# Loading the first expert group ahead of the routing, its rows from ranks alone, and a shorter last job in a two-block kernel

## The chip, the cores and the metric

The kernel runs on one core of one Trainium2 chip. The metric is device time in microseconds (us). The kernel before takes 1078.39 us, the median of 3 runs (1076.84 to 1080.43). The engines are named as in the profile: PE is TensorE (PEld its weight loads), DVE is VectorE, ACT is ScalarE, POOL is GpSimd, SP is SyncE, which here issues nearly all transfers ("SPq" is its queue). TensorE's clock is shown as a share of full speed: 1.0 is 2.4 GHz and 0.5 is 1.2 GHz.

## The reference, cut to what matters

Two blocks run one after the other on 256 tokens of 1024 channels, everything in float32. The first (retention, gated recurrence, feed-forward) is not touched. The second is a mixer and a mixture of 32 experts:

```python
def second_block(x, ...):
    h = h + hybrid_mixer(rms_norm(h, norm1_g), ...)   # mLSTM half and gMLP half, then y @ w_out
    h = h + hierarchical_moe(rms_norm(h, norm2_g), ...)
    return rms_norm(h, final_g)

def hierarchical_moe(xn, w_rg, b_rg, w_re, b_re, w_gate, w_up, w_down):
    g_sel = argmax(softmax(xf @ w_rg + b_rg))            # 1 of 4 groups per token
    top_p, top_i = top_k(softmax(le of that group), 2)   # 2 of its 8 experts
    weights = p_gsel * top_p / sum(top_p)
    # per expert: (silu(x @ w_gate) * (x @ w_up)) @ w_down, times the weight, summed per token
```

The mixer's output is the concatenation of an mLSTM part (y_m) and a gMLP part (y_g), multiplied by w_out (1024 x 1024). Each expert has w_gate and w_up of 1024 x 512 and w_down of 512 x 1024, 6 MiB together; all 32 make 192 MiB.

## The kernel before, in words

**The mixer's last product (proj8, L316).** w_out is walked in 8 units of 24 products (L331). Each unit's weights come as a raw tile and are split into a high part (whi, on ACT, L159) and a low part (wlo, on DVE, L165), so that three fast products give float32 accuracy; `unit` (L204) makes the splits of the units ahead before its own products, with 4 whi and 3 wlo buffers. Units 0 to 3 use the y_m half. In the middle of unit 3 PE transposes the y_g half (`mid_yg`, L1316, transposes L1236). Its evacuation into a high and a low part (ACT L1244, DVE L1245) is called before unit 4 (`before_wo`, L1320), so behind the splits of unit 4 on ACT's queue. Engines run their queues in program order.

**The routing (L1425 to L1530).** From the logits, chains of small DVE steps pick the group and two experts of each token (EB marks them, L1452). PE counts: `ranks` (L1413) gives each token's rank inside its expert, `counts` the tokens per expert. DVE turns counts into an order of experts (key, then c_pos, their place), PE spreads the places over tokens (L1461), and the "name" of a token's row (512 times place, plus rank) is summed into DD (L1466, L1468) and DB (L1522). `choose` (L1502, L1503) makes a 0/1 matrix of a group's names, and `gather` multiplies it with the normalised tokens (L1510) to line up the rows of a group. Only later `r_ids` (L1539 to L1541) writes IDS, the experts' numbers in order of place, which the transfers need.

**The expert jobs.** Places 28 to 31 belong to experts 0 to 3 whatever the counts (STAT, "static"); the other 28 experts are sorted and known only through IDS. `slot_groups` makes 10 groups of 128 rows, most of four experts with 32 rows. A group g has six jobs: (g, 0) to (g, 3) multiply by w_gate and w_up (`gate_up`, L1627), (g, 4) and (g, 5) by the two column halves of w_down (`down`, L1647) and add to the residual (e0, e1: L1656, L1657, L1663 to L1665). Group 0 holds the four static experts. The jobs stand in the order (0,0) (0,1) (0,2) (0,3) (1,0) (0,4) (0,5) (1,1) ...

**The loads.** One load is one expert's share of one job, 1 MiB. `loads` (L1004) lists them in the order of the jobs: 16 static loads for (0,0) to (0,3), and then (1,0), which needs IDS. `ex` (L1030) issues them in that order and stops at the first load that has no buffer or no IDS yet. There are 18 buffers at the start (L1018 to L1026): four raw2, FR2, FR3, xg, yy, lb, five raw, FR1, two pairs of whi, one pair of wlo. xg and yy are used once, the others again as soon as a job has read them. The last job (9,5) is cut in two halves of 256 columns, whose loads are cut too; each half reads 256 of every 512 columns, that is runs of 1 KiB (L1064, L1065). In the last job the products go part by part (L1646), and `e0`, `e1` split the result in high and low parts.

**Side work.** `chain` queues small steps; after each job `advance(3)` takes one step of each of the first three chains that may run. "rows" has six steps (name rows and weights by token), and "flag" and "fing" (final gain rows) follow prep1.

Of the kernel before, what the change touches and what calls it, by code (L numbers as in the profile page):

```python
# [22 lines left out]
T = 256  # L23
# [16 lines left out]
HOLD = 5  # L40
HOLD_AT, OVER_AT = (3, 1), (3, 2)
# [56 lines left out]
def _build(tc, nc, h, out, ctx, dbg, stop):  # L98
# [105 lines left out]
    def unit(mm, stages=(), n=1, before=None, tag=None):  # L204
# [111 lines left out]
    def proj8(xh, xl, stages, before=None, n=1, mid=None):  # L316

        ps = {}
        for i in range(8):
# [15 lines left out]
            unit(mm, st_, n, before=(before or {}).get(i), tag=("p8", i - 4) if i >= 4 else None)  # L335
# [668 lines left out]
    loads = [(p, c) for g, c in jobs for p in keys[g]]  # L1004
# [25 lines left out]
    def ex(n=len(loads)):  # L1030

        while est["n"] < min(n, len(loads)):
# [27 lines left out]
            w = 2048 // len(t)  # L1060
            for j, b in enumerate(t):
                y = src[:, j * w:j * w + w]
                if (x, c) in last:
                    f = slice(256, 512) if half else slice(0, 256)  # L1064
                    y, b = [z.rearrange("p (m c) -> p m c", c=512)[:, :, f] for z in (y, b)]  # L1065
                SP.dma_start(b, y, cond=has)
# [8 lines left out]

    def raw_of(x, c):
# [5 lines left out]
        return lambda a, b: cols_of(eraw[i], a, b)  # L1082
# [194 lines left out]
    def logits(i):  # L1277

        p = lg["p"]
        for m in (2 * i, 2 * i + 1):  # L1280
# [4 lines left out]
    def squares_of(i):  # L1285

        for t in range(2):
            for j in range(2):
# [27 lines left out]
    def mid_yg():  # L1316
        need("yg")
        yt[0]()

    def before_wo(i):  # L1320
        def f():
            ex(RING2 + 2)
            if i == 4:
                yt[1]()
                yt[2]()
# [6 lines left out]
          mid={(3, 2): mid_yg, (7, 2): mid_wo})  # L1332
# [46 lines left out]
    onB = PD.tile([128, 128], BF16, name="onB")  # L1379
    w1, w2, gs = [sc[:, :, i] for i in range(3)]  # L1380
    DD = PD.tile([128, 4], F32, name="DD")
    d1, d2 = DD[:, 0:2], DD[:, 2:4]
    LGg, LGe = LG[:, :, 0:4], LG[:, :, 8:40]
# [11 lines left out]
    dg = H1[:, 4:6, 0:T]  # L1395
# [17 lines left out]
    def ranks(p):  # L1413

        for n, (a, b, c) in enumerate(((triB, 0, 0), (onB, 0, 32), (triB, 1, 32))):
            PE.matmul(p[:, c:c + 32], a, EB[:, b], start=n == 0, stop=False, skip_group_check=True)
# [6 lines left out]


    G.tensor_tensor(triB, tri, ident, op=OP.subtract)  # L1425
    G.memset(onB, 1.0)
    V.tensor_tensor(sqt2[0], sqt2[0], sqt2[2], op=OP.add)
    hs[3][0](lg["h"])
    S.activation(sqt2[3], HT3, AF.Square)
    squares_of(0)  # L1430
    logits(3)
# [554 lines left out]
```

## Time and profile before

| what | value |
|---|---|
| median of 3 runs | 1078.39 us |
| the profiled execution | 1078.93 us, its span 1077.2 us |
| granted PE clock, mean | 0.954 |
| busy share of the span | PE 90%, PEld 71%, DVE 49%, ACT 38%, POOL 7% |
| bytes in the records of transfers, bytes read by the HBM counter | 294.96 MB, 305.16 MB |

The page's three rows on the span, in 40 equal slices (26.9 us each), in which the digits are tenths:

```
PE   6999999999999999999999987999588778878765
PEclk9999999999999999999999988999799988989888
DMA  8545453346456555554664739999999999999994
```

Up to slice 24 PE is busy throughout and the transfers about half of the time; from there to the end the transfers are at their full rate and PE has gaps. In a timeline row stand the start, the time, the engine, the line, the operation, output and inputs, the number of records merged, and in brackets the idle time ahead and what ended it. A float32 product appears as two records.

### The profile page before, as it was taken

The numbers are of one execution on the slowest core, as the hardware profiler recorded it, in microseconds if no ns is written. First come the engines' busy times: TensorE is split into PE (matmuls) and PEld (weight loads), VectorE is DVE, ScalarE is ACT, GpSimd is POOL, SyncE is SP. The second block draws the span as 40 slices with busy tenths as digits, with TensorE's granted clock in tenths as the row PEclk, the third lists the DMA queues.
The fourth block names the chain that finished last, engine by engine and source line by source line (L and its number), as shares of the span: only waits on it lengthen the run. The fifth ranks groups of instructions, "written<-read, shape, count | busy, mean of one in ns | idle before, by whom it ended". The sixth has DMA issues, their size and how long they took to land.

```text
span 1077.2 us, 19357 instructions
## 1 busy us (share of the span) xinstructions
PE 972.0 (90%) x7815; PEld 763.7 (71%) x7815; DVE 532.7 (49%) x961; ACT 405.8 (38%) x675; POOL 71.1 (7%) x59
## 2 busy tenths in 40 slices
PE   6999999999999999999999987999588778878765
PEld 6999998899999999999978964545244424424322
DVE  6787784476777666567877533313112202112012
ACT  6567954366465544445486431111001000100002
POOL 2037500010000000000200000000000000000001
PEclk9999999999999999999999988999799988989888
DMA  8545453346456555554664739999999999999994
GB/s 334 187 165 185 144 195 115 111 154 208 184 195 218 192 195 176 178 195 162 229 234 154 317 127 418 417 413 417 412 420 417 415 421 417 417 419 417 416 407 152
DMA packets 51482, 294.96 MB, mean 274 GB/s; under 512 B 5429, under 2 KB 11189, under 8 KB 20666
## 3 DMA queue, kind: packets, MB, share of 16 engines
q1 hardware_dynamic: 51096, 293.25, 70.1%
q8 instruction: 64, 1.05, 0.4%
q10 hardware_dynamic: 290, 0.39, 0.2%
q14 instruction: 32, 0.26, 0.1%
HBM read 305.16 MB, written 1.05 MB: 284 GB/s over the span
## 4 chain that ended last, share of the span: by engine, by line
PE 62%; DMA 30%; DVE 4%; ACT 1%; issue 1%; SPq 1%; ACTq 0%; DVEq 0%
PE mm L227 42%; DMA raw<-in_we_dram 13%; DMA FR<-in_we_dram 7%; DMA whi<-in_we_dram 6%; PE mm L331 4%; PE sa L1627 3%; PE mm L1647 3%; DMA wlo<-in_we_dram 2%; PE tp L1510 2%; DMA lb<-in_we_dram 2%; PE tp L227 1%; DVE wlo L165 1%; DMA XS<-in_xt_dram 1%; PE sa L227 1%; PE tp L511 0%
## 5 line engine op out<-in xcount | busy, mean ns | idle before, releaser
L227 PE MATMUL mm<-FR,whi 128*128 128x256 f32 (+1 forms) x2080 | 380.6, 285 | 9.1 <-ACT FR L268 8.0
L227 PEld LDWEIGHTS mm<-FR,whi 128*128 128x128 f32 x2080 | 323.4, 190 | 11.9 <-ACT FR L268 8.0
L165 DVE TENSOR_TENSOR wlo<-raw,whi 128x1024 fp32r<-128x1024 f32 x188 | 243.9, 1300 | 139.6 <-PE mm L227 72.0
L227 PE MATMUL mm<-FR,wlo 128*128 128x256 f32 (+1 forms) x1040 | 295.3, 284 | 0.8 <-DVE wlo L165 0.8
L159 ACT ACTIVATE whi<-raw 128x1024 fp32r<-128x1024 f32 x190 | 200.3, 1059 | 201.7 <-PE mm L227 142.2
L227 PEld LDWEIGHTS mm<-FR,wlo 128*128 128x128 f32 x1040 | 198.0, 190 | 1.0 <-DVE wlo L165 1.0
L1627 PE MATMUL sa<-raw,xg 128*32 128x256 f32 (+1 forms) x1200 | 150.6, 426 | 19.5 <-DMA raw<-in_we_dram 19.5
L1627 PEld LDWEIGHTS sa<-raw,xg 128*32 128x32 f32 (+1 forms) x1200 | 73.2, 126 | 56.4 <-DMA raw<-in_we_dram 27.2
L1647 PE MATMUL mm<-raw,ht 128*32 128x512 f32 (+2 forms) x328 | 73.0, 638 | 14.3 <-DMA raw<-in_we_dram 14.3
L1627 PE MATMUL sa<-FR,xg 128*32 128x256 f32 (+1 forms) x416 | 71.6, 426 | 15.7 <-DMA FR<-in_we_dram 15.7
L1638 ACT ACTIVATE ht<-tp 128x128 f32<-128x128 f32 x40 | 11.1, 278 | 173.5 <-PE tp L1637 173.5
L1627 PE MATMUL sa<-whi,xg 128*32 128x256 f32 (+1 forms) x256 | 67.8, 422 | 2.6 <-DMA whi<-in_we_dram 2.6
L1657 DVE SCALAR_TENSOR_TENSOR yy<-mm,ws,yy 128x512 fp32r<-128x512 f32 (+1 forms) x21 | 15.2, 724 | 110.2 <-ACT yy L1656 110.2
L1665 DVE TENSOR_TENSOR XS<-mm,XS 128x512 f32<-128x512 f32 (+1 forms) x42 | 26.0, 661 | 84.5 <-PE mm L1664 84.5
L1627 PEld LDWEIGHTS sa<-FR,xg 128*32 128x32 f32 (+1 forms) x416 | 33.2, 126 | 36.2 <-DMA FR<-in_we_dram 20.7
L1647 PEld LDWEIGHTS mm<-raw,ht 128*32 128x32 f32 (+1 forms) x328 | 18.4, 122 | 56.9 <-issue 28.6
L1633 DVE TENSOR_TENSOR sg<-sg,sa 128x128 f32<-128x128 f32 x40 | 11.3, 283 | 81.2 <-ACT sg L1632 81.2
L227 PE MATMUL mm<-FL,whi 128*128 128x256 f32 x176 | 49.9, 284 | 0.0
L331 PE MATMUL mm<-FR,whi 128*128 128x256 f32 x256 | 48.5, 290 | 1.6 <-ACT FR L1244 1.4
L227 PE MATMUL mm<-FH,wlo 128*128 128x256 f32 x176 | 49.8, 283 | 0.0
L227 PE MATMUL mm<-FH,whi 128*128 128x256 f32 x176 | 49.8, 283 | 0.0
L1510 PE MATMUL tp<-qm,FR 128*128 128x256 f32 (+1 forms) x192 | 42.9, 377 | 1.8 <-DVE qm L1503 1.8
(427 smaller groups left out, 1400.1 us busy)
## 6 DMA issues: line engine op xcount, KB each, us to landing
raw<-in_we_dram SPq DMA_DIRECT2D x106, 1024.0 KB
raw<-in_wd_dram SPq DMA_DIRECT2D x94, 1024.0 KB
FR<-in_we_dram SPq DMA_DIRECT2D x35, 1024.0 KB
whi<-in_we_dram SPq DMA_DIRECT2D x44, 512.0 KB
lb<-in_we_dram SPq DMA_DIRECT2D x12, 1024.0 KB
wlo<-in_we_dram SPq DMA_DIRECT2D x22, 512.0 KB
raw<-in_we_dram SPq DMA_DIRECT2D x4, 512.0 KB
raw<-in_wd_dram SPq DMA_DIRECT2D x2, 512.0 KB
```

The source lines that it names most:

```text
L159: S.activation(his[u], half(u), AF.Copy)
L165: (G if u in POOL_LO or u - 2 * nch in POOL_LO else V).tensor_tensor(los[u], half(u), his[u].bitcast(F32), op=OP.subtract)
L227: PE.matmul(o, a, b, start=start and i == 0, stop=stop and i == 2)
L331: PE.matmul(p[:, j * T:j * T + T], w[:, b:b + 128], z[:, k, 0:T], start=k == 0 and j == 0 and x == 0, stop=k == 7 and x == 2, skip_group_c ...
L1510: PE.matmul(p[:, kk * 256:kk * 256 + w], XN[:, t, k * 128:k * 128 + 128], qm[:, t, 0:w], start=t == 0, stop=t == 1)
L1627: PE.matmul(p[r, 0:256], x[:, k, r], raw(k * 256, k * 256 + 256), start=k == 0, stop=k == 7)
L1633: V.tensor_tensor(sg[:, 128:256], sg[:, 0:128], p[:, 128:256], op=OP.mult)
L1638: S.activation(ht()[:, c], q[:, 0:128], AF.Copy)
L1647: PE.matmul(p[r, 0:n], ht[:, m, r], raw(m * 512 + a, m * 512 + a + n), start=m == 0, stop=m == 3)
L1657: V.scalar_tensor_tensor(yl, p[:, 0:n], ws[:, 0:1], yh.bitcast(F32), OP.mult, OP.subtract)
L1665: V.tensor_tensor(HB[:, t, c0:c0 + n], o[:, 0:n], HB[:, t, c0:c0 + n], op=OP.add)
```

## The change

It has these parts. (1) **Load order**: the four static loads of (0,4) are moved ahead of (1,0); the order of the jobs stays. (2) **First group's rows from ranks alone**: the places of the static experts are constants (BS), so PE adds them to the ranks directly, and `names` makes the row names of group 0 in DS before places are known; keys, places and the names of the other groups follow behind the first matrices (`places` ahead of the first gather product, `places_mm` after the second), and the first group's gathered rows are all evacuated by ACT. (3) **Unread products**: `turn` lets PE multiply 128 x 256 constants into a tile that nobody reads, three times ahead of the ranks and twice behind the counts. (4) **gMLP part**: `mid_yg` also evacuates the y_g half, and unit 3 leaves the splits of its last unit ahead (`defer`) until after its products. (5) **End of w_out**: the last addition, square and logits go in two halves. (6) **Name rows in three steps** instead of six; flag and fing wait for prep2 and prep3. (7) **Last job**: products go k-step by k-step over the four experts; of the second half two experts come ahead of the first half's additions and two behind; the second half skips the split and uses one exact float32 product. The second half of w_down lies in memory as two blocks of 256 columns, so each half load is one run of 4 KiB per partition. (8) **Output**: one of four output transfers is issued by ACT.

```diff
-    def unit(mm, stages=(), n=1, before=None, tag=None):
+    def unit(mm, stages=(), n=1, before=None, tag=None, defer=0):
...
-        for i in range(u, u + NHI):
-            split_hi(i)
-            if i < u + NLO:
-                split_lo(i)
+        def split(a, n):
+            for i in range(u + a, u + n):
+                split_hi(i)
+                if i < u + n - NHI + NLO:
+                    split_lo(i)
+        split(0, NHI - defer)
         if before:
             before()
         mm(his.pop(u), los.pop(u))
+        if defer:
+            split(1, NHI)
...
-    loads = [(p, c) for g, c in jobs for p in keys[g]]
+    begun = list(jobs)
+    begun.insert(begun.index((1, 0)), begun.pop(begun.index((0, 4))))
+    loads = [(p, c) for g, c in begun for p in keys[g]]
...
     def mid_yg():
         need("yg")
-        yt[0]()
+        for f in yt:
+            f()
...
-                yt[1]()
-                yt[2]()
                 need("x1")
...
+    def turn(n):
+        for _ in range(n):
+            PE.matmul(pr["t"][:, 0:256], ident, CS, start=True, stop=True)
...
+    p = pr["s"] = ps_ga()
+    for j in range(2):
+        PE.matmul(p[:, 32 * j:32 * j + 32], onB, BS, start=j == 0, stop=False, skip_group_check=True)
+    turn(TURN[0])
+    ranks(p, False)
...
+    names(DS.rearrange("p w j -> p (w j)"), p)
     p = pr["p"] = ps_ga()
     ranks(p)
     counts(p)
+    turn(TURN[1])
...
-    r_db(d1, d2)
-    for f in gather(0):
+    gs0 = gather(0)
+    gs0[0]()
+    places()
+    for i, f in enumerate(gs0[1:]):
+        if i == 2:
+            places_mm()
         f()
...
-    chain(seq(r_ids, r_exp), hb_ev, r_w, lambda: r_diag((w1, w2), dg), lambda: r_row(DR[:, 2:4], dg),
-          lambda: r_diag((d1, d2), dg), lambda: r_row(DR[:, 0:2], dg), tag="rows")
+    chain(seq(r_ids, r_exp, lambda: r_diag((d1, d2), dg)),
+          seq(lambda: r_row(DR[:, 0:2], dg), r_w, lambda: r_diag((w1, w2), dg2), hb_ev),
+          lambda: r_row(DR[:, 2:4], dg2), tag="rows")
...
-        e0, e1 = down(hts[g], parts, *prep[g], 512, 256)
+        mm, e0, e1 = down_steps(hts[g], *prep[g], 512, 256)
+        mm(parts)
         squares(0, 0, 512)
         gain(0, 512)
         e0()
+        mm_, e0_, e1_ = down_steps(hts[g], *prep[g], 768, 256, exact=True)
+        mm_(parts[:2])
         e1()
+        mm_(parts[2:])
         squares(1, 512, 256)
         gain(512, 256)
-        return down(hts[g], parts, *prep[g], 768, 256)
+        return e0_, e1_
```

**SP's queue at the routing.** These rows are SP's queue from the sixteenth load on, in the kernel before; each DMA row is a load or half of one (a pair of whi tiles takes one load), TENSOR_LOAD reads IDS, and the ISA rows prepare the registers.

```order
L1066 DMA raw_6873<-in_we_dram 128x2048
L1066 DMA FR1_6875<-in_we_dram 128x2048
L1066 DMA whi_6877<-in_we_dram 128x1024
L1066 DMA whi_6878<-in_we_dram 128x1024
L1051 TENSOR_LOAD IDS_6897
L1051 ISA x2
L1052 TENSOR_LOAD IDS_6897
L1052 ISA x2
L1066 ISA
L1066 DMA whi_7087<-in_we_dram 128x1024
```

And the same stretch in the changed kernel.

```order
L1072 DMA raw_6873<-in_we_dram 128x2048
L1072 DMA FR1_6875<-in_we_dram 128x2048
L1072 DMA whi_6877<-in_we_dram 128x1024
L1072 DMA whi_6878<-in_we_dram 128x1024
L1072 DMA whi_6881<-in_we_dram 128x1024
L1072 DMA whi_6882<-in_we_dram 128x1024
L1072 DMA wlo_6885<-in_we_dram 128x1024
L1072 DMA wlo_6886<-in_we_dram 128x1024
L1072 DMA raw2_6082<-in_we_dram 128x2048
L1072 DMA raw2_6211<-in_we_dram 128x2048
L1061 TENSOR_LOAD IDS_6906
```

Four loads (two in whi and wlo pairs, two in raw2 tiles that the first job has read) now stand ahead of the first read of IDS.

**ACT's queue in w_out.** In the kernel before, ACT makes the high parts of units 4 to 7 (whi) and then evacuates the transposed y_g half (FR0).

```order
L1214 ACTIVATE rs2_6078<-rs2_6078,VT_69 128x16
L159 ACTIVATE whi_6626<-raw_6335 128x1024
L159 ACTIVATE whi_6658<-raw_6335 128x1024
L159 ACTIVATE whi_6687<-raw_6381 128x1024
L159 ACTIVATE whi_6726<-raw_6381 128x1024
L1244 ACTIVATE FR0_6461<-tp_6702,VT_69 128x256 x2
L1244 ACTIVATE FR0_6461<-tp_6707,VT_69 128x256 x2
```

In the changed kernel:

```order
L1225 ACTIVATE rs2_6078<-rs2_6078,VT_69 128x16
L160 ACTIVATE whi_6626<-raw_6335 128x1024
L160 ACTIVATE whi_6658<-raw_6335 128x1024
L1255 ACTIVATE FR0_6461<-tp_6698,VT_69 128x256 x2
L1255 ACTIVATE FR0_6461<-tp_6703,VT_69 128x256 x2
L160 ACTIVATE whi_6730<-raw_6381 128x1024
L160 ACTIVATE whi_6734<-raw_6381 128x1024
```

The evacuation has moved ahead of the splits of units 6 and 7; on DVE the low parts of units 5, 6 and 7 have moved behind it in the same way.

**PE's queue in the last job.** In the kernel before, mm_11218 is the first half of the columns and mm_11255 the second; raw_6871, raw_6873, FR1 and whi hold the four experts.

```order
L1647 MATMUL mm_11218<-raw_6871,ht_11042 32x256 x4
L1647 MATMUL mm_11218<-raw_6873,ht_11042 32x256 x4
L1647 MATMUL mm_11218<-FR1_6875,ht_11042 32x256 x4
L1647 MATMUL mm_11218<-whi_6877,ht_11042 32x256 x2
L1647 MATMUL mm_11218<-whi_6878,ht_11042 32x256 x2
L1663 MATMUL mm_11242<-yy_7494,pm_10935 128x256
L1664 MATMUL mm_11242<-yy_7494,pm_10935 128x256
L1663 MATMUL mm_11246<-yy_7494,pm_10935 128x256
L1664 MATMUL mm_11246<-yy_7494,pm_10935 128x256
L1647 MATMUL mm_11255<-raw_6871,ht_11042 32x256 x4
```

In the changed kernel, from the last products of the second half's first two experts (mm_11270) to the first ones of its last two; ahead of these rows the first half (mm_11246) goes through the four experts in turn, four times.

```order
L1711 MATMUL mm_11270<-raw_6871,ht_11072 32x256
L1711 MATMUL mm_11270<-raw_6873,ht_11072 32x256
L1740 MATMUL mm_11279<-yy_7503,pm_10963 128x256
L1741 MATMUL mm_11279<-yy_7503,pm_10963 128x256
L1740 MATMUL mm_11283<-yy_7503,pm_10963 128x256
L1741 MATMUL mm_11283<-yy_7503,pm_10963 128x256
L1711 MATMUL mm_11270<-FR1_6875,ht_11072 32x256
L1711 MATMUL mm_11270<-whi_6878,ht_11072 32x256
```

The four experts, which use different column groups of the array, now alternate, and half of the second half's products stands ahead of the first half's additions (mm_11279, mm_11283).

## Rows read from the trace of the kernel before

**Rows 1.** Chain that ended last: start us, us, what; the stage of the loads.

```profile
701.83 12.48 DMA whi<-in_we_dram
...
1030.20 19.89 DMA raw<-in_we_dram
```

**Rows 2.** Windows: stretch, busy us (records) by engine, PEclk, DMA share, GB/s.

```profile
624.00:626.00 2.00, 0.96 (x11) 0.80 (x10) 1.05 (x7) 0.00 (x0) 0.00 (x0) 1.00 0.79 303
626.00:640.00 14.00, 12.22 (x133) 9.62 (x136) 3.67 (x17) 3.75 (x7) 0.00 (x0) 0.76 0.01 3
640.00:644.00 4.00, 4.00 (x80) 2.44 (x76) 3.16 (x14) 2.68 (x7) 0.00 (x0) 1.00 0.58 178
644.00:648.00 4.00, 4.00 (x53) 2.50 (x49) 0.76 (x3) 0.45 (x2) 0.00 (x0) 1.00 0.83 309
...
700.00:1046.00 346.00, 278.81 (x2306) 129.75 (x2294) 63.45 (x166) 30.06 (x95) 0.00 (x0) 0.90 1.02 417
1046.50:1058.00 11.50, 8.91 (x51) 2.88 (x52) 2.75 (x6) 3.05 (x6) 0.00 (x0) 1.00 0.98 325
```

**Rows 3.** Timeline of SP: issues around the routing, and the last output.

```profile
618.42 0.90 SPq L1066 DMA_DIRECT2D whi<-in_we_dram  x2
...
640.35 0.89 SPq L1066 DMA_DIRECT2D whi<-in_we_dram  x2
...
1073.21 0.46 SPq L1837 DMA_DIRECT2D out_dram<-XS  x1
```

**Rows 4.** Waits of SP from 618 to 646: total us, times, longest.

```profile
SPq L1051 <- DVE IDS L1541: 19.2, 1, 19.2
```

**Rows 5.** Timeline of PE, from w_out to the second gather.

```profile
601.85 0.91 PE L331 MATMUL mm<-FR,whi 128*128 128x256 f32 x2 [1.44 <-ACT FR L1244]
...
627.85 6.66 PE L1510 MATMUL tp<-qm,FR 128*128 128x128 f32 x32 [1.78 <-DVE qm L1503]
634.44 3.66 PE L1627 MATMUL sa<-raw,xg 128*32 128x256 f32 x64
...
645.48 1.89 PE L1510 MATMUL tp<-qm,FR 128*128 128x256 f32 x8
```

**Rows 6.** Timeline of ACT at w_out's fourth unit.

```profile
600.38 1.06 ACT L159 ACTIVATE whi<-raw 128x1024 fp32r<-128x1024 f32 x1 [1.70 <-issue]
```

**Rows 7.** Windows where PE idled or its clock was low.

```profile
603.00:606.00 3.00, 3.00 (x15) 2.88 (x15) 1.22 (x3) 0.66 (x2) 0.00 (x0) 0.50 1.00 423
622.70:624.30 1.60, 0.03 (x1) 0.00 (x0) 1.46 (x11) 1.24 (x3) 0.00 (x0) 1.00 0.96 269
627.00:632.00 5.00, 4.15 (x19) 4.09 (x20) 1.83 (x7) 0.14 (x1) 0.00 (x0) 0.50 0.00 0
```

**Rows 8.** Timeline of DVE, end of w_out to IDS.

```profile
618.24 0.69 DVE L1296 TENSOR_TENSOR H<-mm,H 128x512 f32<-128x512 f32 x1 [3.44 <-PE mm L331]
...
624.08 0.23 DVE L1452 TENSOR_TENSOR EB<-XS 128x64 bf16<-128x64 f32 x1
624.80 0.20 DVE L1457 TENSOR_SCALAR kc<-tp,VT 32x1 f32<-32x1 f32 x1 [0.50 <-PE tp L1422]
...
626.18 0.27 DVE L1466 TENSOR_TENSOR VT<-XS,tp 128x128 f32<-128x128 f32 x1
...
626.80 0.29 DVE L1522 TENSOR_TENSOR DB<-DD,IO 128x32 f32<-128x32 f32 x2
...
638.37 0.21 DVE L1541 CAST IDS<-tp 1x64 int32<-1x64 f32 x1 [4.21 <-PE tp L1540]
```

**Rows 9.** Chain that ended last, the tail.

```profile
1050.14 3.63 PE mm L1647 x26
...
1056.28 4.54 PE mm L1647 x32
...
1062.51 4.54 PE mm L1647 x32
...
1068.60 0.77 DVE XS L1665 x2
```

More of the change, by code (lines that the diff above doesn't have):

```diff
@@ L1059, in ex @@
                 has = None
[L1060 to L1066, printed above, removed]
+            w = 1024 if (x, c) in last else 2048 // len(t)
+            for j in [half] if (x, c) in last else range(2048 // w):
+                SP.dma_start(cols_of(t, j * w, j * w + w), src[:, j * w:j * w + w], cond=has)
             if not half:
@@ L1379, in _build @@
     onB = PD.tile([128, 128], BF16, name="onB")
+    BS = PD.tile([128, 32], BF16, name="BS")
     w1, w2, gs = [sc[:, :, i] for i in range(3)]
@@ L1410, in top, with ranks @@
             V.max_index(i[:, t], m[:, t], x[:, t])
-    def ranks(p):
+    def ranks(p, first=True):
         for n, (a, b, c) in enumerate(((triB, 0, 0), (onB, 0, 32), (triB, 1, 32))):
-            PE.matmul(p[:, c:c + 32], a, EB[:, b], start=n == 0, stop=False, skip_group_check=True)
+            PE.matmul(p[:, c:c + 32], a, EB[:, b], start=first and n == 0, stop=False, skip_group_check=True)
     def counts(p):
@@ L1641, in down, with down_steps, product, mm @@
     def down(ht, parts, pm, ws, c0, n):
+        mm, e0, e1 = down_steps(ht, pm, ws, c0, n)
+        mm(parts)
+        return e0, e1
+    def down_steps(ht, pm, ws, c0, n, exact=False):
         p = ps_dn()
-        a = c0 % 512
-        for m, (raw, r) in [(m, e) for m in range(4) for e in parts] if n == 512 else \
-                [(m, e) for e in parts for m in range(4)]:
-            PE.matmul(p[r, 0:n], ht[:, m, r], raw(m * 512 + a, m * 512 + a + n), start=m == 0, stop=m == 3)
+        def product(raw, r, m):
+            x, y = ht[:, m, r], p[r, 0:n]
+            if c0 < 512:
+                PE.matmul(y, x, raw(m * 512, m * 512 + 512), start=m == 0, stop=m == 3)
+            elif n == 512 and len(raw.t) == 1:
+                w = raw.t[0].rearrange("p (q m c) -> p q m c", q=2, m=4)[:, :, m]
+                PE.matmul(two(y), x, w, start=m == 0, stop=m == 3)
+            else:
+                for q in range(n // 256):
+                    a = (c0 - 512) // 256 * 1024 + q * 1024 + m * 256
+                    PE.matmul(y[:, q * 256:q * 256 + 256], x, raw(a, a + 256), start=m == 0 and q == 0, stop=m == 3,
+                              skip_group_check=True)
+        def mm(parts):
+            for m in range(4):
+                for raw, r in parts:
+                    product(raw, r, m)
         y = {}
@@ L1654, in e0 @@
             n_y[0] += 1
+            if exact:
+                y[0] = fl(PD.tile([128, 2, T], F32, name="sg", bufs=2))[:, 0:n]
+                S.activation(y[0], p[:, 0:n], AF.Copy, scale=ws[:, 0:1])
+                return
             yh, yl = y[0], y[1] = B["Y4"][:, i, 0:n], B["Y4"][:, i + 1, 0:n]
@@ L1791, in _build @@
     launch()
-    chain(r_flag, tag="flag", after=["rows", "prep1"])
-    chain(fing_row, lambda: None, lambda: fing_rows(0), lambda: fing_rows(1), tag="fing", after=["rows", "prep1"])
+    chain(r_flag, tag="flag", after=["rows", "prep2"])
+    chain(fing_row, lambda: None, lambda: fing_rows(0), lambda: fing_rows(1), tag="fing", after=["rows", "prep3"])
     for g, c in jobs:
```

99 lines of the change are left out of this document (64 added, 35 removed).

## Prediction

> **What bounds the kernel now.** I read four views in turn. The page's 40 slices first: up to about 620 us PE is full, from about 650 us to the end the transfers are. The chain of waits says the same: from 701.83 on nearly every piece is PE waiting for a load, with a few of a job's last products between, until the loads end near 1050 [rows 1]. The windows by stage then show that from 700 to 1046 the transfers are at share 1.02 and 417 GB/s, while PE's 278.8 us of work have 346 us of room [rows 2]. So the end of the kernel is: the moment at which the stream of loads runs again after the routing, plus the bytes that are left, plus a tail. The stream stands still in between: its share is 0.79, 0.01, 0.58 and 0.83 in the windows 624 to 626, 626 to 640, 640 to 644 and 644 to 648, which is 2 x 0.21 + 14 x 0.99 + 4 x 0.42 + 4 x 0.17 = 16.6 us lost [rows 2]. The timeline and the waits of SP give the reason: the last static load is issued at 618.42, then SP waits 19.2 us for IDS, and the next load goes out at 640.35 [rows 3, 4]. Whatever shortens this gap moves the end by the same amount, so long as the stream stays full behind it.
>
> One load is 1.049 MB. At 417 GB/s, raised by 305.16/294.96 because the HBM counter saw more bytes than the records hold, it takes 2.43 us.
>
> **The change, part by part.**
>
> *Load order.* SP's queue now has four more loads ahead of the IDS read. Two go to pairs of whi and wlo that w_out has left, like the pair at 618.42, so they need no wait: 2 x 2.43 = 4.9 us of the gap are filled. If those buffers came too late it would be 0; I take 4.9. The other two go to tiles that job (0,0) reads, and wait for its products. That wait stands ahead of the IDS read and of every later load, but it ends no later: (0,0) ends at 634.44 + 3.66 = 638.10, IDS is written at 638.58 [rows 5, 8]. These two are issued about 0.1 us after (0,0), where the first load that needs IDS came 2.25 us after it (640.35), since SP reads and prepares registers first. Restart 2.1 us earlier, bounds 0 and 2.3.
>
> *gMLP part.* PE idles 1.44 us at 601.85 for the high part of y_g [rows 5]; ACT was at a split of a later unit, itself 1.70 us late because its whi buffer was still being read [rows 6]. Behind that pause the granted clock is 0.50 from 603 to 606 [rows 7], 1.5 us lost. Both go: 2.9, and about 0.4 at the clock's edges, so 3.3 us. What is late next is the low part of unit 5, now behind the evacuation on DVE; I count it just in time, since unit 4's 24 products cover it. Bounds 1.4 (the clock falls all the same) and 3.9.
>
> *End of w_out.* The addition of 0.69 us [rows 8] lets PE start after half of it: 0.3 us, bounds 0 and 0.5.
>
> *Names from ranks.* From the end of EB (624.31) to the first gather product (627.85) are 3.54 us. What stays is ranks to DVE, 0.49 (to 624.80); product and sum of names, 0.62 (626.18 to 626.80); and from there to PE 1.05 less about a quarter for DB, 0.8 [rows 5, 8]. That is 1.9, so 1.6 us gained, bounds 1.2 and 2.0. The steps on keys, places and counts are the same instructions behind it; DVE has room for them while PE gathers.
>
> *Unread products and the gather.* The gather's 32 records take 6.66 us [rows 5], at a granted clock of 0.50 from 627 to 632, after a stretch (622.7 to 624.3) in which PE was busy 0.03 of 1.6 us [rows 7]. At full clock 8 records of twice the width take 1.89 us [rows 5], so 32 of these 32 x 1.89 / 16 = 3.8 us. The five unread products (10 records, 2.4 us) stand in PE's pauses around the ranks. But the gather now has pauses of its own: all evacuations are ACT's, and the third of its four parts waits for the places to leave their tile. I add 1.3 us for them, so 5.1 instead of 6.6: 1.5 us gained. Bounds: at the low clock with the same pauses 1.3 us lost; without pauses 2.8 gained.
>
> *Sum for the stream.* PE's path is 3.3 + 0.3 + 1.6 + 1.5 = 6.7 us shorter, the restart 2.1 earlier beyond that, and 4.9 are filled: 13.7 of the 16.6 us. The low ends together give 1.3, the low ends of the four PE terms with the loads as taken 8.3, and the high ends are cut off at 16.6.
>
> *Name rows in three steps, flag, fing.* They take PE's time while the stream runs at full share. PE has 16 circulating buffers of lead to lose before SP would wait for it, so I cost them at nothing, as long as the share in 650 to 700 stays near 1.0; without that cover it is a few us.
>
> *Last job.* From the last load of (9,4) at 1050.14 to the first of the last additions at 1068.60 are 18.46 us [rows 9]. Up to the first half's products (1056.28) nothing changes: 6.14. These then took 4.54, one expert after the other; the same number of records at twice the width took 3.63 where four experts alternate [rows 9], so half of it, 1.8. The second half's 16 + 16 records have two experts alternating: each half of them takes between 0.9 (a quarter of 3.63) and 2.3 (half of 4.54), I take 1.75 for each, with 0.6 for the first half's additions between them. Then ACT, 0.5 with its start, and one exact product of two records, 2 x 0.24 from the 1.89 row, with 0.3 for hand-overs. Sum 6.14 + 1.8 + 1.75 + 0.6 + 1.75 + 0.5 + 0.5 + 0.3 = 13.3, so 5.1 us gained, bounds 3 and 6.5. In the output the fourth issue at 1073.21 [rows 3] loses one of its predecessors on SP, 0.4 us. ACT's issue costs ACT nothing that is waited for. Tail: 5.5.
>
> The half loads themselves run at 325 GB/s against 417 before [rows 2]; in runs of 4 KiB I expect the 417. They have then landed before PE asks for the last two experts, about 10.3 us behind (9,4), so this gives nothing by itself; at the old 325 GB/s PE would wait up to 1.2 us there. The Trainium skill, "DMA: Bandwidth & Descriptors", section Specifications, puts the smallest transfer for full rate at 512 B; by that rule runs of 1 KiB are at full rate already and the new layout changes nothing in the rate. The trace doesn't agree: 325 beside 417 at a share of 0.98.
>
> **Sum.** 13.7 + 5.5 = 19.2 us off the profiled 1078.93 (its span of 1077.2 and 1.7 around it) is 1059.7. The median is 0.54 under the profiled execution, so 1059.2; I round up for small waits to 1059.5 us.
>
> **Rivals.**
>
> *The clock falls in the routing all the same* (chance 0.18). For it: after only 1.44 us of pause it fell at 603, and the gather has pauses. Against it: five more products. The gather's term turns from 1.5 gained to 1.3 lost: 1062.3.
>
> *The gMLP part gives little* (0.09), because unit 5 waits for its low part and the clock falls again: 1.4 instead of 3.3, and some of the low part's 1.2 us on top: about 1062.
>
> *The half loads stay at 325 GB/s* (0.05): up to 1.2 us more, 1060.7. This is what the rule above would give.
>
> *The change doesn't do what it says* (0.05): the two early loads come late, because whi and wlo are held longer. Then 4.9 us stay: 1064.4.
>
> *Slower: PE becomes the bound of the loads' stage* (0.03). PE will meet the stream earlier than at 701.83 and pause more, and pauses lower its clock. At clock 0.90 its work takes 278.8 us of 346. At clock c it is 278.8 x 0.90 / c: it fills the stage at c = 0.73 and has eaten the 19 us at c = 0.69, below which the kernel is slower than before; at 0.5 it would be 502 us. Against it: PE waits in this whole stage already and the clock is 0.90.
>
> **How the numbers follow.** The forecast has 0.60. Its own range is about 1056 to 1062, from the tail's bounds and one or two PE terms. The range for 8 in 10 is 1055.5 to 1065.5, so that the first four rivals lie in it. A measurement of this kernel tells about 0.3% from no change. Only the slower rival is above the old time: faster 0.96, within 0.3% 0.01, slower 0.03.
>
> **What will show it.** In the changed profile: the windows of 624 to 650 should hold some 3 us of lost share instead of 16.6; the first raw2 load should be issued near 631, ahead of IDS; PE's pause at the start of w_out's unit 4 should be gone and the clock there at 1.0; the gather should take about 5 us from about 622.6 at clock 1.0; the share should stay at 1.0 up to about 1033; and from (9,4)'s last load to the first of the last additions should be about 13.3 us. A share below 1.0 after 650, or a low clock in the gather, would make the forecast wrong.

## The result, and the profile after

The changed kernel takes 1063.86 us (median of 4 runs, 1063.26 to 1065.13); the kernel before, with one more run beside it, 1079.41 us. The ratio is 0.9857, with a 95% interval of 0.9841 to 0.9874, so it is about 15.5 us faster. The forecast was 1059.5 us: the direction held, and the time is 4.4 us above the forecast, above the forecast's own range of 1056 to 1062 and inside the range for 8 in 10 (1055.5 to 1065.5). The profiled execution took 1063.26 us (span 1061.6), 15.7 us less than the profiled one of before; the forecast was 19.2.

Line numbers below are the changed kernel's where its trace is meant: L1677 are the gate-and-up products, L1704 and L1711 those of w_down, L1439 the unread products, L1460 the transposes, L1555 the gather, L1428 the ranks, L1506 the places.

The chain of waits of the changed kernel at its end (start us, us, what), against [rows 1, 9]:

```profile
1019.17 18.26 DMA raw<-in_we_dram
...
1037.47 5.33 PE mm L1704 x26
...
1045.32 3.58 PE mm L1711 x48
...
1049.56 1.88 PE mm L1711 x16
...
1052.05 0.71 PE mm L1738 x2
...
1052.79 0.43 DVE XS L1742
```

The end is still made of the same pieces: loads, the products of (9,4) behind their last load, the last job, the last additions. (9,4)'s last load comes at 1037.47 instead of 1050.14, 12.7 us earlier. But the 26 records behind it take 5.33 us, where they took 3.63 [rows 9].

Windows of the changed kernel (stretch, busy us of PE, PEld, DVE, ACT and POOL, granted clock, DMA share, GB/s), against [rows 2, 7]:

```profile
618.00:620.50 2.50, 2.50 (x14) 2.44 (x13) 2.33 (x19) 2.16 (x4) 0.00 (x0) 0.50 1.02 423
...
628.00:630.00 2.00, 1.79 (x16) 1.82 (x16) 0.69 (x5) 0.62 (x2) 0.00 (x0) 1.00 0.95 387
630.00:632.00 2.00, 2.00 (x39) 1.19 (x41) 0.00 (x0) 1.72 (x3) 0.00 (x0) 1.00 0.12 43
632.00:634.00 2.00, 2.00 (x43) 1.01 (x36) 0.00 (x0) 0.19 (x1) 0.00 (x0) 1.00 0.00 0
634.00:636.00 2.00, 2.00 (x42) 1.23 (x44) 1.03 (x5) 1.50 (x2) 0.00 (x0) 1.00 0.51 102
636.00:700.00 64.00, 60.68 (x668) 32.73 (x660) 22.38 (x74) 12.30 (x34) 0.00 (x0) 1.00 1.01 417
...
1037.50:1041.00 3.50, 3.50 (x20) 0.99 (x24) 0.00 (x0) 0.00 (x0) 0.00 (x0) 0.51 1.02 408
```

The gap of the stream has shrunk to 2 x (0.05 + 0.88 + 1.00 + 0.49) = 4.8 us, from 16.6, and behind it the share stays at 1.01. The last loads run at 408 GB/s instead of 325. Two of these stretches are at clock 0.50: 618 to 620.5, while PE is full, and 1037.5 to 1041, right behind (9,4)'s last load.

SP of the changed kernel (start us, us, issues), against [rows 3]:

```profile
616.97 2.82 SPq L1072 DMA_DIRECT2D wlo<-in_we_dram  x2
633.83 5.06 SPq L1072 DMA_DIRECT2D raw<-in_we_dram  x4
```

The first of the four raw loads goes out at the end of job (0,0), 6.5 us before the 640.35 of before and before IDS (634.09).

PE of the changed kernel in the routing (start us, us, line, output and inputs, records, idle before and its releaser), against [rows 5]:

```profile
617.16 3.10 PE L1460 MATMUL mm<-CS,H 128*128 128x128 f32 x16
...
620.15 2.04 PE L1439 MATMUL sa<-CS 128*128 128x256 f32 x6
622.03 0.18 PE L1428 MATMUL tp<-EB,triB 128*128 128x32 bf16 x1
...
623.76 1.49 PE L1555 MATMUL tp<-qm,FR 128*128 128x128 f32 x8 [0.18 <-DVE qm L1548]
625.97 1.16 PE L1555 MATMUL tp<-qm,FR 128*128 128x128 f32 x8 [0.71 <-ACT xg L1561]
...
628.21 2.02 PE L1555 MATMUL tp<-qm,FR 128*128 128x128 f32 x16 [0.52 <-DVE VT L1486]
630.16 3.66 PE L1677 MATMUL sa<-raw,xg 128*32 128x256 f32 x64
```

DVE of the changed kernel beside it, against [rows 8]:

```profile
614.83 0.76 DVE L1450 TENSOR_TENSOR H<-mm,H 128x256 f32<-128x256 f32 x2 [3.44 <-PE mm L336]
...
620.45 0.22 DVE L1475 TENSOR_TENSOR EB<-XS 128x64 bf16<-128x64 f32 x1
622.30 0.29 DVE L1486 TENSOR_TENSOR VT<-XS,tp 128x128 f32<-128x128 f32 x1 [1.62 <-PE tp L1428]
```

w_out's last additions begin 3.4 us earlier (618.24 before), although w_out itself begins 0.3 us later (first product at 588.10, before at 587.78). EB is written at 620.67, but the ranks start at 622.03: at the low clock the transposes take 3.10 us, and the three unread products behind them run past EB. So DVE waits 1.62 us. The gather is at clock 1.00, yet takes 6.40 us to the start of (0,0), since each part waits: for ACT to empty the one free tile, then for the places and the names in the other.

### The profile page after: what moved, and what is told of

The parts are those of the page before. It is cut to its first block, busy times and chain, and to the rows that moved or that the text cites. A ratio compares the mean times of both kernels' runs of the same rounds, so it can differ in the third digit from the quotient of the medians.

```text
span 1061.6 us, 19447 instructions
## 1 busy us (share of the span) xinstructions
PE 968.0 (91%) x7862; PEld 760.6 (72%) x7862; DVE 530.8 (50%) x959; ACT 407.6 (38%) x680; POOL 71.5 (7%) x64
## 4 chain that ended last, share of the span: by engine, by line
PE 60%; DMA 33%; DVE 3%; ACT 2%; issue 1%; SPq 0%; ACTq 0%; DVEq 0%
PE mm L232 42%; DMA raw<-in_we_dram 19%; DMA whi<-in_we_dram 6%; DMA FR<-in_we_dram 5%; PE mm L336 4%; PE sa L1677 3%; DMA wlo<-in_we_dram 1%; PE tp L232 1%; PE tp L1555 1%; DVE wlo L166 1%; PE mm L1711 1%; DMA XS<-in_xt_dram 1%; PE sa L232 1%; PE mm L1704 1%; DMA H<-in_rw_dram 0%
## 5 line engine op out<-in xcount | busy, mean ns | idle before, releaser
L1677 PE MATMUL sa<-raw,xg 128*32 128x256 f32 (+1 forms) x1168 | 148.3, 421 | 18.3 <-DMA raw<-in_we_dram 18.3
L1677 PEld LDWEIGHTS sa<-raw,xg 128*32 128x32 f32 (+1 forms) x1168 | 71.1, 126 | 56.3 <-DMA raw<-in_we_dram 26.1
L1677 PE MATMUL sa<-FR,xg 128*32 128x256 f32 (+1 forms) x448 | 79.2, 439 | 17.2 <-DMA FR<-in_we_dram 17.2
L1677 PE MATMUL sa<-whi,xg 128*32 128x256 f32 (+1 forms) x272 | 65.3, 424 | 1.7 <-DMA whi<-in_we_dram 1.7
L1677 PEld LDWEIGHTS sa<-FR,xg 128*32 128x32 f32 (+1 forms) x448 | 36.0, 129 | 36.9 <-DMA FR<-in_we_dram 22.1
L1677 PEld LDWEIGHTS sa<-whi,xg 128*32 128x32 f32 (+1 forms) x272 | 29.4, 126 | 19.5 <-issue 8.4
L1682 ACT ACTIVATE sg<-sa 128x128 f32<-128x128 f32 x40 | 11.1, 276 | 82.9 <-PE sa L1677 70.3
L1707 PE MATMUL mm<-raw,ht 128*32 128x512 f32 (+1 forms) x128 | 33.6, 740 | 8.6 <-DMA raw<-in_we_dram 8.5
## 6 DMA issues: line engine op xcount, KB each, us to landing
lb<-in_we_dram SPq DMA_DIRECT2D x12, 1024.0 KB, 14.9
```

The costliest lines, as they stand in the source:

```text
L1677: PE.matmul(p[r, 0:256], x[:, k, r], raw(k * 256, k * 256 + 256), start=k == 0, stop=k == 7)
L1682: S.activation(sg[:, 0:128], p[:, 0:128], AF.Silu)
L1707: PE.matmul(two(y), x, w, start=m == 0, stop=m == 3)
```

## The experiments

All times are medians with lowest and highest; ratios are to the kernel before in runs on the same chip. The groups of runs were not all on one chip: the kernel before took 1079.41 us beside the changed kernel, 1080.35 beside the four undone parts, 1078.55 beside the runs on the routing and the unread products of (9,4), and 1078.67 beside the last four. So a median set against the changed kernel's 1063.86 is uncertain by some 2 us. The instructions ahead of w_out are the same in all kernels made from the changed one, and yet w_out's last additions begin between 613.6 and 617.2 us in them (the gMLP experiment, which moves them itself, left out); from w_out's first product to these additions are 26.7 or 26.8 us in each, so the spread comes from ahead of w_out. So effects of a few us are read from a stretch of the trace rather than from the total.

Parts 2, 5, 6 and 8 were not undone by themselves; what is said of them is read from the traces.

### The parts, each undone

**Load order as before.**

```diff
-    begun.insert(begun.index((1, 0)), begun.pop(begun.index((0, 4))))
```

> The changed kernel with the loads in the order of the jobs again, so that only 16 loads can be issued ahead of IDS. Theory (the two early loads fill 4.9 us of the gap and the two on (0,0)'s tiles restart the stream 2.1 to 2.25 us earlier, and the end moves by the same amount): 7.1 us slower than the changed kernel's 1063.9, so 1071.0 us; the stretch without transfers begins 4.9 us earlier, and the first load behind it is issued 2.2 us behind IDS instead of at the end of (0,0). Rival (part of the gap is given back, since PE has less to wait for behind it): 3 us or less, 1067 us.

1070.35 us (1067.69 to 1071.04), ratio 0.990 (0.988 to 0.992): 6.5 us above the changed kernel by the medians, 4.6 by the ratios. DMA share in this kernel's windows:

```profile
624.00:626.00 2.00, 1.16 (x8) 0.89 (x8) 0.78 (x6) 0.62 (x2) 0.00 (x0) 1.00 0.36 147
626.00:634.00 8.00, 7.47 (x100) 5.47 (x104) 0.99 (x7) 3.15 (x7) 0.00 (x0) 1.00 0.01 3
634.00:636.00 2.00, 2.00 (x40) 1.20 (x40) 1.00 (x5) 1.60 (x3) 0.00 (x0) 1.00 0.04 12
636.00:638.00 2.00, 2.00 (x34) 0.95 (x22) 1.69 (x9) 0.17 (x1) 0.00 (x0) 1.00 0.39 102
```

Up to 638 that is 1.3 + 7.9 + 1.9 + 1.2 = 12.3 us lost, 7.5 more than in the changed kernel. (9,4)'s last load comes 7.9 us later (1045.41 against 1037.47), with (0,0) at the same time (630.05 against 630.16). So the theory (7.1) holds, and the rival falls. Behind that load the two profiled executions differ in two more things: (9,4)'s 26 records take 3.63 us here instead of 5.33, and PE waits for the last half load until 1057.00, so that from (9,4)'s last load to the first of the last additions are 14.9 us where the changed kernel takes 13.6 at full clock (below). Why this half load comes late is open.

**gMLP part as before** (the later stages of y_g ahead of unit 4, no deferred splits).

```diff
-        for f in yt:
-            f()
+        yt[0]()
...
             if i == 4:
+                yt[1]()
+                yt[2]()
...
-          mid={(3, 2): mid_yg, (7, 2): mid_wo}, defer=(3,))
+          mid={(3, 2): mid_yg, (7, 2): mid_wo})
```

> The changed kernel with the gMLP part as before: the two later stages of y_g ahead of unit 4 and the splits of w_out's unit 3 undivided. Theory (the pause of 1.44 us at the start of unit 4 comes back, and the clock falls behind it): w_out ends 3.4 us later and the kernel takes 1067.3 us. Rival (the clock falls in the routing anyway, and with the fall moved to w_out the routing is at full clock, so about half is given back): 1065.5 us.

1067.23 us (1065.37 to 1068.45), ratio 0.987 (0.985 to 0.989): 3.4 us above the changed kernel by the medians, as the theory says, but 1.6 by the ratios, as the rival says, so the total does not decide. The trace does: from w_out's first product to its last additions are 30.58 us (589.71 to 620.29), in the changed kernel 26.73 (588.10 to 614.83), 3.85 us more. The pause and the clock behind it are back (PE row, then a window):

```profile
603.77 0.90 PE L336 MATMUL mm<-FR,whi 128*128 128x256 f32 x2 [1.45 <-ACT FR L1255]
```

```profile
606.00:608.00 2.00, 2.00 (x11) 2.00 (x11) 0.48 (x1) 0.17 (x1) 0.00 (x0) 0.50 1.01 426
```

In this execution the clock did not fall at the transposes, but in the gather's second half, whose 16 records took 3.66 us instead of 2.02. So what the rival says of the transposes came true, and yet nothing was given back: from w_out's last additions to (0,0) are 15.6 us (620.29 to 635.93) against 15.3.

**Last job's products as before.**

```diff
-        mm(parts)
+        for part in parts:
+            mm([part])
...
         e0()
-        mm_, e0_, e1_ = down_steps(hts[g], *prep[g], 768, 256, exact=True)
-        mm_(parts[:2])
         e1()
-        mm_(parts[2:])
         squares(1, 512, 256)
         gain(512, 256)
-        return e0_, e1_
+        mm, e0, e1 = down_steps(hts[g], *prep[g], 768, 256)
+        for part in parts:
+            mm([part])
+        return e0, e1
```

> The changed kernel with the last job's products as before: expert by expert in each half, the second half behind the first half's additions, and the last product on two rounded parts instead of one exact. The new layout of the second half's weights stays. Theory (from the start of the first half's products to the first of the last additions 12.3 us as before, where the changed kernel takes 7.5): 4.85 us slower than the changed kernel, 1068.7 us. Rival (the products of two experts don't run beside each other and the gain was elsewhere): 1 to 2 us slower, 1065.5 us.

1067.80 us (1065.09 to 1071.42), ratio 0.988 (0.986 to 0.991). Its chain of waits:

```profile
1045.04 4.54 PE mm L1711 x32
...
1051.26 4.54 PE mm L1711 x32
...
1057.35 0.77 DVE XS L1742 x2
```

From the first half's products to the last additions are 12.31 us, against 1052.79 - 1045.32 = 7.47: 4.84 us, the theory's number.

**Runs of 1 KiB as before** in the second half of w_down.

```diff
-            w = 1024 if (x, c) in last else 2048 // len(t)
-            for j in [half] if (x, c) in last else range(2048 // w):
-                SP.dma_start(cols_of(t, j * w, j * w + w), src[:, j * w:j * w + w], cond=has)
+            w = 2048 // len(t)
+            for j, b in enumerate(t):
+                y = src[:, j * w:j * w + w]
+                if (x, c) in last:
+                    f = slice(256, 512) if half else slice(0, 256)
+                    y, b = [z.rearrange("p (m c) -> p m c", c=512)[:, :, f] for z in (y, b)]
+                SP.dma_start(b, y, cond=has)
```

(and the weights' layout and the products' columns to match)

> The changed kernel with the second half of w_down laid out as before, so that the last eight half loads read runs of 1 KiB again; the order of the products stays. Theory (the half loads come at 325 GB/s instead of about 410, so the last lands some 2 us later, but PE asks for it later still): same time, 1063.9 us within 0.5. Rival (the alternating products now ask for it earlier, and PE waits for the last halves): 1 to 2 us slower, 1065.4 us. Second rival (1 KiB is at full rate and the low rate had another cause): 410 GB/s in the last 10 us of the transfers.

1062.49 us (1059.95 to 1064.33), ratio 0.984 (0.982 to 0.986), no slower than the changed kernel: the total does not show the part. The trace does (windows, then PE at (9,4)'s last load and in the last job, then the first of the last additions):

```profile
1034.00:1036.00 2.00, 1.22 (x12) 0.42 (x16) 0.00 (x0) 0.00 (x0) 0.00 (x0) 1.00 0.99 309
1036.00:1038.00 2.00, 2.00 (x18) 0.48 (x10) 0.00 (x0) 0.00 (x0) 0.00 (x0) 1.00 1.00 314
```

```profile
1034.78 0.62 PE L1708 MATMUL mm<-raw,ht 128*32 128x512 f32 x1 [1.50 <-DMA raw<-in_we_dram]
...
1043.78 1.91 PE L1708 MATMUL mm<-raw,ht 128*32 128x256 f32 x14 [0.57 <-DMA raw<-in_we_dram]
```

```profile
1049.58 0.44 DVE XS L1738
```

The rate is back to 310 GB/s, so the layout makes it, and PE now waits for a half load. From (9,4)'s last load (1034.78) to the first of the last additions (1049.58) are 14.8 us; at the same full clock the 4 KiB layout takes 13.6 (1040.31 to 1053.93 in the run below without the first three unread products; the changed kernel's 15.3 less the 1.7 of its low clock is the same). So the new layout is worth 1.2 us, as the first rival had it, but only together with the alternating products, which ask for the halves earlier: with the old order of products the stretch from the first half's products to the last additions is the same in both layouts (12.32 us before, 12.31 in the run above). The total hides it: in this execution the clock fell neither at the transposes nor in (9,4), and w_out ended 1.2 us earlier than in the changed kernel's.

### The routing

**No unread products ahead of the ranks**, and **one instead of three**.

```diff
-TURN = (3, 2)
+TURN = (0, 2)      # the other run: (1, 2)
```

> The changed kernel without the three unread products ahead of the ranks; the two behind the counts stay. Theory (at the low clock the three ran past EB and held the ranks back, 622.03 instead of about 620.7): the ranks come 1.3 us earlier and the kernel takes 1062.6 us. Rival (they are what brought the clock back to full, so that without them the gather runs at 0.50): the gather takes 2 to 3 us more, 1065.5 us.

> The changed kernel with one unread product ahead of the ranks instead of three. Theory (the one ends at about 620.8, hardly behind EB): 1.15 us off, 1062.7 us, with the gather at clock 1.00. Rival (the clock is back later, in the gather): 1064 to 1065 us.

With none: 1061.66 us (1060.23 to 1065.85), ratio 0.985 (0.982 to 0.987). With one: 1062.81 us (1062.32 to 1063.79), ratio 0.986 (0.984 to 0.988). Neither total is told from the changed kernel's. PE with none:

```profile
620.85 0.18 PE L1428 MATMUL tp<-EB,triB 128*128 128x32 bf16 x1 [1.58 <-DVE EB L1475]
```

and its window:

```profile
623.50:632.50 9.00, 7.76 (x34) 7.03 (x32) 1.21 (x9) 1.88 (x6) 0.00 (x0) 0.50 0.75 301
```

Both theories are half right. From EB's start to the first gather product it takes 2.0 us (620.57 to 622.57) instead of 3.3. But PE stood idle for 1.58 us, the clock fell, and from the first gather product to (0,0) are 10.05 us (622.57 to 632.62) instead of 6.40. With one, the clock fell at the transposes again, EB to gather took 2.45 us, and the gather ran at full clock. In all three traces without unread products ahead of the ranks (this one, the kernel before, and the load order alone, at the end) the gather ran at the low clock; in ten of the eleven with three or one of them it ran at full clock, and in the gMLP experiment the clock fell in its second half. So the unread products do hold the clock, though not each time.

**The gather in tiles that don't wait for each other.**

```diff
-        p = ps_ga()
+        p = (ps_gu if act and k2 in (1, 2) else ps_ga)()
```

> The changed kernel with the first gather's second and third parts in the two accumulator tiles of the gate-and-up products, which are free then, so that its parts don't wait for one tile's evacuation and for the names. Theory (the pauses, not the clock, made the gather 6.5 us): 32 records in some 4.4 us, (0,0) ends 2.0 us earlier, 1061.9 us. Rival (the first products of (0,0) wait for the evacuation instead, or the stream does not start earlier): 1063 to 1064 us.

1058.81 us (1058.32 to 1062.33), ratio 0.982 (0.980 to 0.983). PE:

```profile
626.10 1.49 PE L1555 MATMUL tp<-qm,FR 128*128 128x128 f32 x8 [0.18 <-DVE qm L1548]
627.42 1.06 PE L1555 MATMUL sa<-qm,FR 128*128 128x128 f32 x8
628.41 0.63 PE L1506 MATMUL tp<-IO,kc 32*128 32x32 f32 x4
628.97 1.16 PE L1555 MATMUL sa<-qm,FR 128*128 128x128 f32 x8
629.96 1.06 PE L1555 MATMUL tp<-qm,FR 128*128 128x128 f32 x8
630.95 1.29 PE L1677 MATMUL sa<-raw,xg 128*32 128x256 f32 x20
```

4.85 us to (0,0) instead of 6.40: 1.55 us were pauses. The median is 5 us below the changed kernel's, and 4.4 below that of the next run (1063.17), on the same chip; this is more than the 2.0 expected. The profiled execution (1062.33 us, the slowest of the five) explains 0.9 us below the changed kernel's: 1.55 from the gather and 1.7 from (9,4) at full clock, which this edit does not touch, less 2.3 by which w_out ended later. The other executions were not profiled, so the rest of the median's fall stays open.

### The tail

**Unread products where (9,4) waits for its loads**, one ahead of the third expert's first product and three ahead of the fourth's.

```diff
             for m in range(4):
-                for raw, r in parts:
+                for i, (raw, r) in enumerate(parts):
+                    if m == 0 and i < len(fill):
+                        turn(fill[i])
                     product(raw, r, m)
...
+            mm(parts, (0, 0, 1, 3) if g == NG - 1 else ())
```

> The changed kernel with four unread products in job (9,4), one ahead of the third expert's first product and three ahead of the fourth's, where PE waits for loads. Theory (the clock of 0.50 in the products behind (9,4)'s last load comes from these waits): the 26 records behind the last load take 3.6 us instead of 5.3, 1062.2 us. Rival (the clock falls whatever stands there, or the fillers end behind the load): no gain, 1063.9 to 1064.4 us.

1063.17 us (1060.43 to 1063.51), ratio 0.985 (0.983 to 0.987): not told from the changed kernel. Its chain of waits:

```profile
1038.00 1.49 PE sa L1439 x6
1039.49 3.56 PE mm L1704 x26
```

3.56 us, as the theory says. But six of the nine profiled executions that were made from the changed kernel without such products in (9,4) also took 3.6 us; only three took 5.33. With them (here and in the two kernels with both repairs below) three of three took 3.6. That fits the theory and does not prove it. The unread products, not the load, now end last ahead of the 26 records, so they may cost a little; how much was not separated.

### The changed kernel again, both repairs, and the load order alone

> The changed kernel itself once more, beside the two that are made from it. Theory (the products of 40 columns and of one column ahead of the transposes leave the clock near an edge, at which it falls in some executions and not in others): 1062 to 1065 us, with executions that differ by 1 to 3 us; in the profiled one the clock falls at the transposes or it does not, and only where it falls are the ranks more than 0.5 us behind EB. Rival (the 1063.9 us of the first runs are what this kernel takes): 1063.9 us, all runs within 1 us, the clock low at the transposes again.

> The changed kernel with both repairs, the first gather in four tiles that don't wait for one another and four unread products where (9,4) waits for its loads. Theory (1.6 us of pauses leave the gather, and the products of (9,4) never run at the low clock, which cost 1.7 us in the changed kernel's profiled execution): 2 to 3 us below the changed kernel in the same runs, near 1061 us; gather 4.9 us, (9,4) behind its last load 3.6 us. Rival (the low numbers of the run with the tiles alone were chance): no different from the changed kernel in the same runs.

> Both repairs, and one unread product ahead of the ranks instead of three. Theory (the three hold the clock through the gather but are late where the clock falls at the transposes; one is never late by more than 0.6 us): another 0.8 us off where the clock falls at the transposes, near 1060.3 us. Rival (one product is too few where the clock does not fall there, and the gather then runs at the low clock): up to 2.5 us slower than with three, 1062 to 1063.5 us.

| kernel | median us | lowest to highest | ratio (95%) |
|---|---|---|---|
| changed, again | 1063.50 | 1061.74 to 1064.79 | 0.987 (0.984 to 0.989) |
| both repairs | 1058.87 | 1057.20 to 1061.80 | 0.982 (0.980 to 0.985) |
| both, one unread product | 1058.81 | 1057.42 to 1059.29 | 0.982 (0.980 to 0.984) |

The changed kernel's repeat, PE:

```profile
618.85 1.94 PE L1460 MATMUL mm<-CS,H 128*128 128x128 f32 x16
...
620.68 1.54 PE L1439 MATMUL sa<-CS 128*128 128x256 f32 x6
622.42 0.18 PE L1428 MATMUL tp<-EB,triB 128*128 128x32 bf16 x1 [0.19 <-DVE EB L1475]
```

The same instructions, and the clock did not fall here: the transposes take 1.94 us, the unread products end in time, the ranks wait 0.19 us for EB, and EB to gather takes 2.0 us. In all six traces with three unread products and the low clock at the transposes the ranks start 1.1 to 1.4 us behind EB; in the three with the full clock there they wait 0.19 us for it. So the late ranks come from the clock. In (9,4) it was low again, 5.33 us. The theory holds (the five executions differ by 3 us), and the rival, with all within 1 us, falls.

With both repairs the gather takes 4.85 us and (9,4) 3.6 us, in both kernels. Each of the five executions with one unread product lies below each of the changed kernel's five. This is the best version here, about 4.7 us below the changed kernel. In the total one product against three can't be told apart; in the traces, both with the low clock at the transposes, EB to gather takes 2.45 us with one and 3.31 with three, which is the theory's 0.8. The gain of both repairs, 4.6 us, is more than the 2 to 3 expected, and their median is no lower than that of the tiles alone (1058.81, on another chip): the totals show no gain from the unread products in (9,4), and what lies beyond the gather's 1.55 us stays open.

**The load order alone**, in the kernel before.

```diff
-    loads = [(p, c) for g, c in jobs for p in keys[g]]
+    begun = list(jobs)
+    begun.insert(begun.index((1, 0)), begun.pop(begun.index((0, 4))))
+    loads = [(p, c) for g, c in begun for p in keys[g]]
```

> The kernel before with the changed load order alone. Theory (two loads of 2.43 us fill 4.9 us of the gap and the two on (0,0)'s tiles start 2.2 us earlier than the first one behind IDS): 7.1 us faster than the kernel before in the same runs, 1072 us. Rival (without the other parts PE, late by its own gather, gives part of it back behind the gap): 3 to 5 us faster, 1075 us.

1077.26 us (1073.62 to 1081.89, 12 runs) against 1078.67, ratio 0.999 (0.9975 to 1.0005): nearly nothing. The profiled execution, the fastest of the twelve, is 5.3 us below the profiled one of before, but its w_out ended 2.5 us earlier (615.74 against 618.24), which the load order does not move. The theory falls. The rival is right that PE gives the gain back, but it names the gather where the trace shows the flag and fing rows, and its price is far too small. The trace shows where it went (PE; the line numbers are this kernel's: L1551 is the flag, L1587 the rows of fing, L1512 a gather, L1629 gate and up):

```profile
658.99 0.18 PE L1551 MATMUL tp<-ones,kc 32*1 32x1 f32 x2 [5.26 <-DVE jr L1550]
659.12 3.76 PE L1587 MATMUL tp<-H,ones 1*128 1x512 f32 x4
662.81 5.25 PE L1512 MATMUL tp<-qm,FR 128*128 128x256 f32 x16
```

and its windows:

```profile
664.00:668.00 4.00, 4.00 (x17) 3.05 (x15) 0.88 (x2) 0.00 (x0) 0.00 (x0) 0.76 0.91 377
668.00:672.00 4.00, 4.00 (x71) 2.22 (x74) 2.49 (x9) 1.06 (x4) 0.00 (x0) 1.00 0.07 25
672.00:676.00 4.00, 4.00 (x35) 1.34 (x35) 0.29 (x1) 0.83 (x4) 0.00 (x0) 1.00 0.81 283
```

Name rows, flag and fing stand in one stretch here. PE runs no job from 650.67 to 667.99: it waits 5.26 us for the flag's chain on DVE, its clock falls (0.50 from 656 to 664), and the fing rows and the next gather run slowly. SP waits 11.0 us for tiles that PE has not read (its waits: total us, times, longest),

```profile
SPq L1068 <- PE tp L1639: 11.0, 1, 11.0
```

and the stream stands still a second time: 0.4 + 3.7 + 0.8 = 4.9 us. In the kernel before, PE is busy for only 6.9 of the 12 us from 648 to 660 too, but its stream had started later and did not run dry: share 1.01 from 660 to 700.

## Why the prediction was right in direction and 4 us low

**Load order** (4.9 and 2.1): right. (0,0) starts 4.28 us earlier (634.44 to 630.16), the first load behind the gap 6.52 us; the difference, 2.24, is the restart. With the two early loads that is 11.4, and 1.3 more came, most of it because the loads behind the restart ramped up faster (the 0.58 and 0.83 of [rows 2] are gone): 12.7 us at (9,4)'s last load, against the forecast's 13.7.

**gMLP part and end of w_out** (3.3 and 0.3): right. From w_out's first product to its last additions were 30.46 us and are 26.73, 3.73 gained; the last additions begin only 3.41 earlier (618.24 to 614.83), since w_out began 0.32 later in this execution. From there to EB were 5.84 us and are 5.62, 0.22 gained.

**Names from ranks** (1.6): right only where the clock holds. EB to gather went from 3.77 to 3.31 us in this execution, 0.46 gained; in the repeat to 2.0, 1.8 gained. The failed step is "the five unread products stand in PE's pauses": at full clock the three ahead of the ranks do, at the low clock they end 1.4 us behind EB and stand in front of the ranks.

**Unread products and the gather** (1.5): the clock was right, the size wrong. The failed step is the 1.3 us of pauses that I added to 3.8 us of products; it is 6.40 - 3.8 = 2.6. From the first gather product to (0,0) was 6.59 and is 6.40: 0.2 gained. Taking the waits between tiles away gave 1.55 back; 0.56 of the rest are the places' four records, which now stand inside the gather (628.41 to 628.97 in that run) and which I had not counted there. The 1.3 us lost at the low clock were too small as well: the run without the first three unread products took 10.05, 3.5 more than before.

**Name rows, flag, fing** (nothing): true of the sum, and the reason was too short. In the changed kernel the share stays at 1.01 from 636 to 700. But the load order alone gave back most of its 7 us in the stretch of flag and fing rows (neither the later flag and fing with nothing else nor the changed kernel with them as before was tried, so this dependence is read from two traces and not shown by an edit). I priced the parts one by one and did not ask which of them needs another.

**Tail** (5.5): 3.0 (from (9,4)'s last load to the end 28.79 before, 25.79 after). The failed step is "up to the first half's products nothing changes": (9,4)'s 26 records took 5.33 us at the low clock instead of 3.63, 1.7 us. Part of this is chance: six of nine traces without unread products there have 3.63. At full clock the stretch forecast at 13.3 takes 13.6, so the sum over the last job was right. (The 3.63 us that I halved were 26 records, not 32 like the first half; the half was right all the same: in the run without the first three unread products the 32 took 1.75, from 1046.39 to 1048.14.) The output's 0.4 did not come: SP's last issue ends 4.4 us behind the first of the last additions instead of 5.1, but the span ends 8.8 behind it instead of 8.6. Why the last transfers take longer is open.

**Half loads**: the rate came as forecast, and so did the price of the old rate beside the new order of products (up to 1.2 us; 1.2 measured). Runs of 1 KiB moved 309 and 314 GB/s at a share of 0.99 and 1.00, runs of 4 KiB 408. The Trainium skill, "DMA: Bandwidth & Descriptors", section Specifications, has full rate from 512 B on; these rows refute that for these loads, and with it the rival that the rate stays.

**The clock rival** (0.18, 1062.3 us) is what came nearest in time, and that is chance: the fall was in other places than it had, ahead of the ranks and behind (9,4)'s last load, and the gather, where it had it, ran at full clock.

In sum 1.0 us is missing from the stream and 2.5 from the tail, which is the whole of 19.2 - 15.7. The other 0.8 of the 4.4 us lies between profiled execution and median: it was 0.5 above the median before and is 0.6 below it here, and 0.3 had been rounded up.

## What to carry to other kernels

Price a filler at the low clock too: one that fits a pause at full clock stands in front of the next real work when the clock is down. Before pricing a part at nothing, ask which other part's gain rests on it: earlier loads bring only what the reader of their tiles keeps up with. And where executions of one kernel differ by more than an edit is worth, read the edit's own stretch of the trace, not the total.

## What the runs showed of the hardware

The clock fell at the transposes, about 3 us after w_out's last additions began and with PE full throughout (2.50 of 2.50 us from 618 to 620.5 in the changed kernel), in 8 of the 12 profiled executions made from the changed kernel, and not in 4, though the instructions up to there were the same in all but one of them (the gMLP experiment). The parts of the change don't explain it: in the kernel before the 16 transposes took 1.95 us, with the load order alone 3.46. Ahead of them stand products of 40 columns and of one column; whether these have a part in it was not tried.

The Trainium skill, "TensorE: Matmul & The Clock Gate", Part 1, says of a kernel's start that the same kernel can have a different number of slow products from run to run, depending on the phase of the watch on PE. The trace agrees on the difference, here in the middle of the kernel (8 low, 4 full); the phase is seen in no run here.
